# Attention layer with two kinds of heads: how the filling work of the first pair of heads is spread over its units

## The chip, the cores and the metric

The kernel runs on one core of one Trainium2 chip. The metric is device microseconds (us) of one execution, the median of several runs. The core has a matrix engine (TensorE, "PE" in the profile; its weight loads are a row of their own, "PEld"), a vector engine (VectorE, "DVE"), an activation engine (ScalarE, "ACT"), a general engine (GpSimd, "POOL") and a queue engine that issues most transfers ("SP"). Matrix products are written to PSUM, a small memory of banks of 512 columns of fp32 each; the other engines read them from there ("evacuate" them).

## The reference, cut to what matters

One layer over 1024 tokens of width 1024. A normalised and modulated input `u` goes through one projection into queries, keys, values and gates of 16 heads of width 64. Eight heads do stick-breaking attention, eight do forgetting attention; each output is multiplied by a SiLU gate, and an output projection, a residual and a layer norm close the layer. The first pairs of heads, which the change is about, are stick-breaking heads:

```python
z = jnp.einsum('bhqd,bhkd->bhqk', q, k).astype(jnp.float32) * scale
strict = k_pos[None, :] < q_pos[:, None]
log_beta = jax.nn.log_sigmoid(z)
log_keep = jnp.where(strict, jax.nn.log_sigmoid(-z), 0.0)
later = lax.cumsum(log_keep, axis=3, reverse=True) - log_keep
w = jnp.where(strict, jnp.exp(log_beta + later), 0.0)
return jnp.einsum('bhqk,bhkd->bhqd', w.astype(v.dtype), v)
```

A block of 128 queries with number i looks at the keys of blocks 0 to i, so its work grows with i.

## The kernel before, in words

The heads are worked in 8 pairs (p = 0 to 7; pairs 0 to 3 are stick-breaking heads, 4 to 7 forgetting ones). A start phase makes the modulated input and the query, key and gate projections that the first pair needs. Then comes one long loop over 128 *units*: a unit is (pair p, head h of the pair, query block i). In the first four pairs the units run through i = 0 to 7 of head 0, then i = 0 to 7 of head 1. Loop step k does, in this order on TensorE:

1. S k: the scores of unit k (`att_scores`, lines 410 and 411), two matmuls per 512 keys, into the S tile. There is one S tile (two PSUM banks), so S k+1 can only start when ScalarE has read S k twice (lines 430 and 431, the two sigmoids). In step 0 these instructions are put behind the evacuation of the last start product (`last_evac`) by `after(...)`.
2. a first helping of filling work, `fill(want[2 * k + LEAD + 1])`;
3. pv: when both units of a block of 256 queries have been transposed, the product with the values (`att_pv`, line 476), one step after the second of them;
4. T k-2: the transposes of the weights of unit k-2 (`att_transpose`, line 461), i+1 of them, in groups of four per PSUM bank. There are two T banks, taken in turn; a bank is free when ScalarE has copied the high part (line 463) and VectorE has made the low part (line 464);
5. a second helping of filling work, `fill(want[2 * k + LEAD + 2])`.

Between S k and T k-2 of a unit stand two sigmoids on ScalarE, a scan on VectorE that forms the running product of the keep factors (line 436, and line 440 for keys beyond 512) and a product on GpSimd (line 444). GpSimd also splits fetched weights into a high and a low part (lines 124 and 125).

The filling work comes from a chain of generators (`fillers`). Each call of `next(fillers)` issues one small piece; `fill` calls it until the count `done` reaches the wanted number. In pair 0 there are 18 calls (`FILL[0]`):

- call 1 starts the generator and holds no matmul;
- calls 2 to 9 make the values of token blocks 4 to 7 for pairs 0 and 1, two calls for a block, 12 matmuls of 256 columns each (lines 310 to 312);
- call 10 only asks for the weights of the next projection and holds no matmul;
- calls 11 to 18 make the gate projection of pair 1, 6 matmuls of 512 columns in each call (lines 255 to 257);
- beside them, the gate of the residual is made from a sum over partitions: two products (line 715) right behind calls 4 and 5, which use T banks and are evacuated by VectorE (line 716).

The order on TensorE is exactly the program's order (`manual_schedule`). On ScalarE, VectorE, GpSimd and SP the framework orders the instructions itself, by a schedule that it works out from the program and its dependences; edges can be added with `after`. Every tile's reuse waits for all its readers.

`want` is a running sum: each pair's `FILL[p]` calls are shared out over half-units in proportion to a weight. Before, the weight of a unit with query block i is W0 + i + 1 with W0 = 100 in all pairs but the last.

Of the kernel before, what the change touches and what calls it, by code (L numbers as in the profile page):

```python
# [27 lines left out]
def tile_hybrid_layer(  # L28
# [902 lines left out]
    W0 = 100.0  # L931
# [11 lines left out]
    def order(p):  # L943
        if p < 4:
            return [(p, h, i) for h in range(2) for i in range(NB)]
        if p < NPAIR - 1:
            return [(p, h, i) for h in range(2) for i in reversed(range(NB))]
        return [(p, h, i + d) for i in reversed(range(0, NB, 2)) for h in range(2) for d in (1, 0)]
# [1 line left out]
    units = [u for p in range(NPAIR) for u in order(p)]  # L950
    want = [0.0]
    for p in range(NPAIR):
        size = [W0 + u[2] + 1 for u in order(p)]
        if p == NPAIR - 1:
            size = [1] * G7 + [0] * (16 - G7)
        for w in size:
            for _ in range(2):
                want.append(want[-1] + FILL[p] * w / (2 * sum(size)))
# [5 lines left out]
    for k in range(len(units) + LAG + 1):  # L964
        if k < len(units):
# [12 lines left out]
            p, h, i = units[k]  # L978
# [5 lines left out]
        if LAG <= k < len(units) + LAG:  # L984
            u = units[k - LAG]
# [79 lines left out]
```

## Time and profile before

| | before |
|---|---|
| median of 3 runs | 690.2 us (690.01 to 690.37) |
| profiled execution | 689.96 us |
| span from its first to its last instruction | 688.2 us |
| mean granted TensorE clock | 0.998 |
| busy: PE, PEld | 674.0 us (98%), 589.7 us (86%) |
| busy: DVE, ACT, POOL | 453.5 us (66%), 382.1 us (56%), 425.7 us (62%) |

The page and the views that the next part quotes name instructions by engine and line, `out<-in`, with the shape and a count (x2: two in one row); in a timeline row the two numbers are start and duration in us, and a bracket gives the idle time of the engine just before and what released it. A row of the view by stretches has the stretch, its length, the busy time of each engine with the count of instructions, the granted clock and the DMA share.

### The profile page before, as it was taken

What the parts mean: (1) busy time and instruction counts of PE and PEld (TensorE: products, weight loads), DVE (VectorE), ACT (ScalarE), POOL (GpSimd) and SP (SyncE); (2) the same over time, 40 slices, a digit from 0 to 9 for tenths busy, and PEclk for the clock granted to TensorE, in tenths of its full rate; (3) what the DMA queues carried; (4) which work ended last, traced back from release to release, by engine and by line L of the source; (5) the groups of instructions that cost most, each with busy time, mean ns of one, the idle gap of its engine ahead of it and who ended that gap; (6) DMA issues with size and microseconds to landing.
All of it is one profiled execution on the core that took longest, in us unless ns stands there. A gap on an engine that the chain in (4) does not pass through costs nothing.

```text
span 688.2 us, 11786 instructions
## 1 busy us (share of the span) xinstructions
PE 674.0 (98%) x4033; PEld 589.7 (86%) x4033; DVE 453.5 (66%) x924; ACT 382.1 (56%) x862; POOL 425.7 (62%) x555
## 2 busy tenths in 40 slices
PE   8999999999999999999999999999999999999996
PEld 4789898888998888889998888889988889888885
DVE  5985458767657676767675665656665767774645
ACT  5666457856657666666674564655565666531000
POOL 4567978656439565556388897877584364665411
PEclk9999999999999999999999999999999999999999
DMA  8956232112102122112144553454341288143301
GB/s 306 416 233 230 85 108 57 26 40 53 40 9 70 41 55 55 38 47 62 25 136 153 177 160 116 146 163 145 100 143 46 67 293 352 56 155 119 128 32 61
DMA packets 44028, 81.59 MB, mean 119 GB/s; under 512 B 5120, under 2 KB 18752, under 8 KB 43072
## 3 DMA queue, kind: packets, MB, share of 16 engines
q1 hardware_dynamic: 42816, 76.65, 34.0%
q10 hardware_dynamic: 1152, 4.19, 2.2%
q8 instruction: 32, 0.52, 0.3%
q14 instruction: 28, 0.23, 0.1%
HBM read 60.34 MB, written 16.29 MB: 111 GB/s over the span
## 4 chain that ended last, share of the span: by engine, by line
PE 92%; DVE 3%; DMA 2%; POOL 1%; issue 1%; ACT 0%; SPq 0%; POOLq 0%; DVEq 0%
PE m L255 10%; PE pv L476 10%; PE m L256 10%; PE m L257 10%; PE T L461 9%; PE S L411 5%; PE S L410 5%; PE o L848 4%; PE o L846 4%; PE o L847 4%; PE v L310 4%; PE v L312 4%; PE v L311 4%; DMA wss<-in_w_ss_dram 1%; DMA x<-in_x_dram 1%
## 5 line engine op out<-in xcount | busy, mean ns | idle before, releaser
L255 PE MATMUL m<-uh,whi 128*128 128x512 f32 x304 | 126.4, 416 | 0.5 <-DVE kl L243 0.5
L256 PE MATMUL m<-ul,whi 128*128 128x512 f32 x304 | 119.8, 394 | 0.0
L257 PE MATMUL m<-uh,wlo 128*128 128x512 f32 x304 | 119.6, 394 | 0.0
L464 DVE TENSOR_TENSOR pt<-T,pt 128x512 fp32r<-128x512 f32 (+2 forms) x192 | 100.5, 550 | 17.9 <-ACT pt L463 16.8
L444 POOL TENSOR_TENSOR be<-be,kp 128x127 f32<-128x127 f32 (+3 forms) x64 | 77.1, 1205 | 33.5 <-DVE kp L440 23.6
L463 ACT CAST pt<-T 128x512 fp32r<-128x512 f32 (+2 forms) x192 | 85.7, 480 | 16.7 <-PE T L461 13.0
L436 DVE TENSOR_TENSOR_SCAN kp<-kp,floor 128x512 f32<-128x512 f32 (+2 forms) x64 | 65.1, 1018 | 32.1 <-ACT kp L430 31.3
L476 PEld LDWEIGHTS pv<-pt,v 128*128 128x128 f32 (+1 forms) x640 | 77.2, 163 | 4.5 <-DVE pt L464 0.7
L476 PE MATMUL pv<-pt,v 128*128 128x256 f32 (+3 forms) x640 | 80.5, 271 | 0.5 <-DVE pt L464 0.5
L425 POOL TENSOR_SCALAR a<-a,l 128x1024 f32<-128x1024 f32 (+3 forms) x64 | 47.9, 748 | 39.5 <-DVE l L424 25.9
L423 ACT ACTIVATE a<-a,nm 128x1024 f32<-128x1024 f32 (+3 forms) x64 | 49.8, 778 | 34.0 <-DVE nm L417 33.0
L257 PEld LDWEIGHTS m<-uh,wlo 128*128 128x128 f32 x304 | 57.1, 188 | 13.5
L410 PE MATMUL S<-k,q 128*128 128x512 f32 (+5 forms) x192 | 66.5, 348 | 0.2 <-DVE nm L417 0.2
L411 PE MATMUL S<-kl,qz 128*128 128x512 f32 (+5 forms) x192 | 65.5, 342 | 0.0
L255 PEld LDWEIGHTS m<-uh,whi 128*128 128x128 f32 x304 | 57.3, 188 | 9.2 <-DVE kl L243 0.9
L256 PEld LDWEIGHTS m<-ul,whi 128*128 128x128 f32 x304 | 57.4, 189 | 8.0
L497 POOL TENSOR_TENSOR ty<-ty,sg 64x256 f32<-64x256 f32 x64 | 47.4, 741 | 24.6 <-DVE ty L496 12.2
L417 DVE CUSTOM_DVE_ANT_0 a<-S,fb 128x1024 f32<-128x1024 f32 (+3 forms) x64 | 48.3, 755 | 20.4 <-PE S L411 9.8
L430 ACT ACTIVATE kp<-S 128x128 f32<-128x128 f32 (+3 forms) x64 | 41.7, 651 | 31.8 <-PE S L411 28.3
L310 PE MATMUL v<-whi_v,uh 128*128 128x256 f32 (+1 forms) x192 | 56.0, 292 | 0.7 <-DVE kl L243 0.7
L388 ACT CAST qz<-q 64x128 fp32r<-64x128 f32 x128 | 37.4, 295 | 33.0 <-PE S L411 31.9
L312 PE MATMUL v<-wlo_v,uh 128*128 128x256 f32 (+1 forms) x192 | 54.2, 282 | 0.0
(291 smaller groups left out, 1611.5 us busy)
## 6 DMA issues: line engine op xcount, KB each, us to landing
raw<-in_w_qkg_dram SPq DMA_DIRECT2D x38, 256.0 KB, 2.8
wss<-in_w_ss_dram SPq DMA_DIRECT2D x7, 1024.0 KB, 8.3
x<-in_x_dram SPq DMA_DIRECT2D x8, 512.0 KB, 7.3
k<-k SPq DMA_DIRECT2D x32, 128.0 KB, 2.5
wg<-in_w_gate_dram SPq DMA_DIRECT2D x8, 512.0 KB, 4.4
raw_o<-in_w_out_dram SPq DMA_DIRECT2D x16, 256.0 KB, 2.7
fb<-f_dr ACTq DMA_DIRECT2D x8, 512.0 KB, 4.2
wo_dr<-whi_o SPq DMA_DIRECT2D x16, 256.0 KB, 2.5
```

Source lines behind the costliest of these rows:

```text
L255: nc.tensor.matmul(acc, hi[:, c], u_hi[kt][:, s], start=(kt == 0), stop=False)
L256: nc.tensor.matmul(acc, hi[:, c], u_lo[kt][:, s], start=False, stop=False)
L257: nc.tensor.matmul(acc, lo[:, c], u_hi[kt][:, s], start=False, stop=(kt == NB - 1))
L310: nc.tensor.matmul(acc[:, :n], u_hi[kt][:, ts_], hi[:, s], start=(kt == 0), stop=False)
L312: nc.tensor.matmul(acc[:, :n], u_hi[kt][:, ts_], lo[:, s], start=False, stop=(kt == NB - 1))
L410: nc.tensor.matmul(S[:, s, :w], qst[p][h][:, qs], kst[p][h][:, ks], start=True, stop=False)
L411: nc.tensor.matmul(S[:, s, :w], z, klo[p][:, ks], start=False, stop=True)
L436: scan = nc.vector.tensor_tensor_scan(rv, rv, floor[0][:, 512 - n:][:, ::-1], initial=0.0, op0=ALU.mult, op1=ALU.max)
L444: nc.gpsimd.tensor_tensor(be[:, :ke - 1], be[:, :ke - 1], kp[:, 1:ke], op=ALU.mult)
L463: nc.scalar.copy(hi[:, :n, qo:qo + P], t3)
L464: nc.vector.tensor_tensor(lo[:, :n, qo:qo + P], t3, hi.bitcast(F32)[:, :n, qo:qo + P], op=ALU.subtract)
L476: nc.tensor.matmul(acc[:m, q0:256], vt[p][:, kb, h * P:h * P + m], pt[:, kb % 4, q0:], start=start, stop=stop)
```

## The change

One expression: in pair 0 the weight of a unit is 4 + i + 1 in place of 100 + i + 1. Over one head the weights then run from 5 to 12 in place of 101 to 108. The 18 calls of the pair stay, and so do all other pairs.

```diff
     for p in range(NPAIR):
-        size = [W0 + u[2] + 1 for u in order(p)]
+        size = [(W0 if p else 4.0) + u[2] + 1 for u in order(p)]
         if p == NPAIR - 1:
```

`fill` works in whole calls, so the places of the calls follow from the running sums ("a": the helping behind the scores, "b": the helping behind the transposes of the step):

| step k | 0 | 1 | 2 | 3 | 4 | 5 | 6 | 7 | 8 | 9 | 10 | 11 | 12 | 13 | 14 |
|---|---|---|---|---|---|---|---|---|---|---|---|---|---|---|---|
| before, a | 1, 2 | | | | 7 | 8 | 9 | | | | | | 16 | 17 | 18 |
| before, b | 3 | 4 | 5 | 6 | | | 10 | 11 | 12 | 13 | 14 | 15 | | | |
| after, a | 1, 2 | | | 5 | 6 | 7 | 9 | 10 | 11 | | | 14 | 15 | 16 | 18 |
| after, b | | 3 | 4 | | | 8 | | | | 12 | 13 | | | 17 | |

From step 15 on the calls stand where they stood (19 and 20 at 15a, 21 at 15b).

## The prediction

> **What bounds the kernel now.** I read the busy times by stretch first, to see which engine has no room, and looked at the stage of the first pair of heads (92.0 to 132.49 us, from the first score product of unit 0 to that of unit 14). Columns: stretch, its length, busy PE, PEld, DVE, ACT, POOL (instructions), clock, DMA.
>
> ```profile
> 92.00:132.49 40.49, 39.17 (x273) 36.03 (x271) 30.82 (x52) 29.78 (x73) 27.42 (x41) 1.00 0.22 60
> 145.00:300.00 155.00, 154.26 (x962) 137.75 (x961) 104.26 (x172) 99.65 (x225) 90.95 (x128) 1.00 0.17 45
> 300.00:500.00 200.00, 200.00 (x1315) 181.85 (x1315) 129.29 (x303) 117.62 (x284) 145.27 (x168) 1.00 0.40 121
> 500.00:620.00 120.00, 119.26 (x690) 102.98 (x689) 84.61 (x217) 69.96 (x170) 67.81 (x86) 1.00 0.48 161
> ```
>
> TensorE (PE) is busy 39.17 of 40.49 us in this stage and practically always from 145 to 620 us. Its work is the same before and after the change. So any new PE gap here is paid in full at the end, because nothing behind it has room to take it back (0.74 us idle in each of two stretches of 155 and 120 us), and all that can be won is the gaps that stand here now. The second view is the timeline of PE around those gaps, in loop step 7 and 8 (S k: scores of unit k; T k: its transposes; columns: start, us, engine, line).
>
> ```profile
> 111.15 0.39 PE L410 MATMUL S<-k,q 128*128 128x512 f32 x1
> 111.38 0.40 PE L411 MATMUL S<-kl,qz 128*128 128x512 f32 x1
> 112.56 0.84 PE L461 MATMUL T<-ident,be 128*128 128x128 f32 x6 [0.78 <-DVE pt L464]
> 113.16 0.47 PE L255 MATMUL m<-uh,whi 128*128 128x512 f32 x1
> ...
> 114.64 0.22 PE L410 MATMUL S<-k,q 128*128 128x128 f32 x1
> ...
> 114.81 0.75 PE L476 MATMUL pv<-pt,v 128*128 128x256 f32 x5
> 116.10 0.98 PE L476 MATMUL pv<-pt,v 128*64 128x256 f32 x7 [0.54 <-DVE pt L464]
> 116.92 0.93 PE L461 MATMUL T<-ident,be 128*128 128x128 f32 x7
> 117.60 0.48 PE L255 MATMUL m<-uh,whi 128*128 128x512 f32 x1
> ```
>
> Matmul records overlap, so I count from start to start: a 128x512 matmul takes 0.23 (111.15 to 111.38), a call of six 1.48 with the refill behind transposes (113.16 to 114.64), a pv product 0.12 ((116.92-116.10)/7). The gap shown as 0.78 is then 112.56-111.38-0.23 = 0.95, the one shown as 0.54 is 116.10-114.81-5 x 0.117 = 0.70. Both wait for VectorE (DVE), whose rows say why:
>
> ```profile
> 110.29 1.01 DVE L440 TENSOR_TENSOR_SCAN kp<-kp,floor 128x384 f32<-128x384 f32 x1
> ...
> 111.73 0.87 DVE L464 TENSOR_TENSOR pt<-T,pt 128x512 fp32r<-128x512 f32 x2
> ...
> 114.18 1.28 DVE L440 TENSOR_TENSOR_SCAN kp<-kp,floor 128x512 f32<-128x512 f32 x1
> 115.38 0.99 DVE L464 TENSOR_TENSOR pt<-T,pt 128x512 fp32r<-128x512 f32 x2
> ```
>
> T 5 needs a T bank that the low part of T 4 frees, and this stands behind the scan of S 6; pv of block 2 needs the low part of T 5, which stands behind the scan of S 7. These scans start when S 6 and S 7 have run. The most that could be won is 0.95 + 0.70 = 1.65.
>
> **The change, part by part.** It adds and removes no instruction; it moves the calls of the filling generator by the table above. Calls 3 to 8 and 11 to 17 come up to a unit later, calls 1, 2, 9 and 18 stand where they stood. Call 10 holds no matmul, so step 7 loses its only cover and step 8 keeps one.
>
> *Step 0 loses call 3.* Behind S 0 only call 2 is left, and then comes S 1, which needs the single S tile: both sigmoids of unit 0 must have read it.
>
> ```profile
> 92.18 0.33 PE L310 MATMUL v<-v_home,uh 128*128 128x256 f32 x1
> ...
> 93.67 0.28 PE L310 MATMUL v<-whi_v_2b,uh 128*128 128x256 f32 x1
> ...
> 95.09 0.28 PE L410 MATMUL S<-k,q 128*128 128x256 f32 x1
> ```
>
> ```profile
> 93.54 0.58 ACT L240 CAST k<-st_k1b 64x512 fp32r<-64x512 f32 x1 [0.55 <-DVE kl L243]
> 94.14 0.28 ACT L430 ACTIVATE kp<-S 128x128 f32<-128x128 f32 x1
> 94.32 0.27 ACT L431 ACTIVATE be<-S 128x128 f32<-128x128 f32 x1
> ...
> 106.11 0.81 ACT L431 ACTIVATE be<-S 128x768 f32<-128x768 f32 x1
> ...
> 112.73 1.02 ACT L431 ACTIVATE be<-S 128x1024 f32<-128x1024 f32 x1
> ```
>
> ```profile
> 106.96 0.47 PE L410 MATMUL S<-k,q 128*128 128x448 f32 x1
> ...
> 110.14 0.71 PE L461 MATMUL T<-ident,be 128*128 128x128 f32 x5
> 110.60 0.48 PE L410 MATMUL S<-k,q 128*128 128x512 f32 x1
> ```
>
> Call 2 ends at 93.67 (the row there is the first matmul of call 3). ScalarE (ACT) reads S 0 late, because the evacuation of the last start product stands ahead of it, put there in the code (the scores of unit 0 follow last_evac), and ends at 94.32+0.27 = 94.59. From such an end to PE go about 0.05 us: the sigmoid from 106.11 ended at 106.92, S 6 began at 106.96. So S 1 starts at 94.64 where PE is free at 93.67: **+0.97**. Before, call 3 covered it (S 1 at 95.09). Bounds: 0 if ACT took the sigmoids ahead of the evacuation, which the code's order excludes; 1.0 with the whole wait.
>
> *Calls 4 to 8 later, the gate products with 4 and 5.* Each of the steps 1 to 4 still has a call between one S and the next, which hides the sigmoids. The gate products now take their T banks in the order T 0, gate, gate, T 1; call 5 stands ahead of the second, so their evictions (one DVE operation each) are hidden; without that cover it would cost one:
>
> ```profile
> 99.81 0.68 DVE L716 SCALAR_TENSOR_TENSOR gate<-bg,gate 128x512 f32<-128x512 f32 x1
> ...
> 118.23 1.16 DVE L464 TENSOR_TENSOR pt<-T,pt 128x512 fp32r<-128x512 f32 x2 [0.24 <-ACT pt L463]
> ```
>
> T 2 needs the GpSimd (POOL) product of unit 2, which stood behind weight splits that waited for a DMA:
>
> ```profile
> 102.93 0.86 POOL L444 TENSOR_TENSOR be<-be,kp 128x383 f32<-128x383 f32 x1
> ```
>
> ```profile
> 102.27 0.28 PE L310 MATMUL v<-whi_v_2b,uh 128*128 128x256 f32 x1
> ...
> 103.69 0.57 PE L476 MATMUL pv<-pt,v 128*128 128x256 f32 x4
> 104.10 0.49 PE L461 MATMUL T<-ident,be 128*128 128x128 f32 x3
> ```
>
> PE now reaches T 2 without call 7 (103.69-102.27 = 1.42) and 0.97 late: 104.10-1.42+0.97 = 103.65. The product ends at 103.79, with 0.05 on it 103.84: **+0.19**, or 0 if POOL takes it ahead of the splits, which this trace cannot show. I take 0.19, since the DMA that holds POOL does not depend on the calls. What POOL queues behind it (products of units 3 and 4) is needed later.
>
> *Calls 7 and 8 on the other side of T 3, call 10 in step 7.* From S 6 to T 5 the PE order is as before, so the 0.95 gap at T 5 stays: the scan of S 6 still starts when S 6 has run.
>
> *Call 11 from behind T 5 to behind S 8.* On the clock of the old trace, T 5 ends at 113.16 and S 8 follows at once, but the sigmoid of unit 7 reads the S tile until 112.73+1.02 = 113.75: S 8 at 113.80, a new gap of 0.64. Then S 8 (114.81-114.64 = 0.17), call 11 (6 x 0.23 = 1.40) and five pv products (0.59) end at 115.96, before the low part of T 5 is there for 116.10. The old gap of 0.70 shrinks to 0.14 and the pv goes on at 116.10 as before: **0** in sum.
>
> *Call 12 from behind T 6 to behind T 7.* This takes the cover from the T banks.
>
> ```profile
> 119.08 0.28 PE L410 MATMUL S<-k,q 128*128 128x256 f32 x1
> ...
> 119.32 1.04 PE L461 MATMUL T<-ident,be 128*128 128x128 f32 x8
> 120.11 0.48 PE L255 MATMUL m<-uh,whi 128*128 128x512 f32 x1
> ...
> 121.59 0.34 PE L410 MATMUL S<-k,q 128*128 128x384 f32 x1
> ...
> 121.94 1.94 PE L476 MATMUL pv<-pt,v 128*128 128x256 f32 x16
> ...
> 132.49 0.47 PE L410 MATMUL S<-k,q 128*128 128x448 f32 x1
> ```
>
> S 9 starts at 117.60 instead of 119.08, and T 7 could start 0.24 later (119.32-119.08), at 117.84. Its bank is freed by the low part of T 6, which DVE starts at 118.23 (row above); the first of the two takes 0.67 (the one from 115.38 let the pv go on at 116.10): with 0.05 on it 118.95, a gap of 1.11. The second bank comes at 118.23+1.16+0.05 = 119.44, so T 7 ends, half of 120.11-119.32 later, at 119.84, call 12 (1.48) at 121.32, S 10 (121.94-121.59 = 0.35) at 121.67. The old order stood at this pv at 121.94 with call 13 (121.59-120.11 = 1.48) done, the new one still owes it: 121.67-121.94+1.48 = **+1.21**. Bounds: 0 if DVE had T 6's parts out by 117.84, which the ACT copy ahead of it excludes; above by one more call without cover, 1.48. Calls 13 to 17 each stand again between two score products, and at S 14 (132.49 before) the debt is paid and the orders are equal.
>
> The sum: 0.97 + 0.19 + 0 + 1.21 = 2.37. The profiled execution took 689.96, so 692.33, say 692.3; it is 0.24 below the median of 690.2, inside their spread, so the median may come out at 692.5.
>
> **Rivals.**
>
> *Only the first wait stays.* ACT and DVE reorder around S 9 so that T 7 finds its banks free: 689.96+0.97+0.19 = 691.1. For it: DVE was idle 0.24 ahead of T 6's low part, so it follows PE closely. Against it: the transposes themselves end only at 117.60, and copy and subtraction must follow.
>
> *The old gaps close (the other side).* With S 6 later against T 3 and T 4, DVE could take the low parts of T 4 and T 5 ahead of the scans of S 6 and S 7; then 0.95 and 0.70 go, T 7's bank is early too, and the first waits remain: 689.96-1.65+1.16 = 689.5. The decisive point is whether the low part of T 4 stands ahead of the second scan of unit 6 on DVE. Against it: that scan started at 110.29, and T 4 ran only from 110.14 to 110.60, with ACT's copy to follow.
>
> *More room than the gaps show.* Weight loads are busy 36.03/40.49 = 89.0% of this stage, and 181.85/200.00 = 90.9% of the stretch without a gap. At that share the stage would take 36.03/0.909 = 39.6, 0.9 less: 689.1, if the new places of the calls also closed the small losses behind transposes. Against it: as many calls as before stand next to transposes or scores. The Trainium skill (Perfetto Trace Analysis, Identifying the Most-Contended Engine) has such a rule: matmul busy share is no good measure of headroom, the weight-load share is. By it the 0.9 would be the headroom in place of the 1.65 counted from start to start; the trace has gaps with a named cause, so I go by these.
>
> *A further wait.* A call moved once more loses its cover, at S 12 for instance, where the tanh of the gate path enters ACT after call 14: up to one call, 1.48, on top: 693.8.
>
> **How the numbers follow.** My forecast 0.60 (its own range 691.6 to 693.2), only the first wait 0.18, a further wait 0.12, old gaps close 0.06, more room 0.04. The range from 690.2 to 694.0 leaves out the two faster cases and a rest above. A change of 0.2% is 1.38 us, about what a measurement of this kernel tells from none. Slower by more than that: most of 0.60, 0.12, and a little of the second case: 0.73; within it: 0.22; faster: 0.05.
>
> **What would show it.** Right: S 1 starts right behind the sigmoid of unit 0, about 1 us of PE idle with ACT as its releaser; a PE gap of about 0.6 ahead of S 8 and of about 1.1 ahead of T 7 (released by DVE), S 14 some 2.4 us later than 132.49, and the same distance at all later units. Wrong: PE runs through from S 0 to T 4 without a gap; the 0.95 at T 5 shrinks; or S 14 moves by 2.4 and the end doesn't, which would mean room behind that I don't see.

## The result, and the profile after

| | before | after |
|---|---|---|
| median (6 runs each, same chip) | 690.24 us (690.01 to 690.62) | 692.54 us (692.24 to 692.81) |
| span of the profiled execution | 688.2 us | 691.1 us |

The ratio is 1.0034 (95% interval 1.0024 to 1.0044): the changed kernel is 0.34% slower, 2.30 us.

The first view is TensorE's own waits in the changed kernel, from 90 to 150 us (line waiting, releaser, us in total, times, longest):

```profile
PE T L461 <- DVE pt L464: 1.8, 2, 1.0
PE S L410 <- ACT be L431: 1.2, 2, 0.8
```

Before, there was no wait of the scores for the sigmoid in this stage; for VectorE there were two at the transposes, 0.9 together and 0.8 of it at T 5, and one of 0.5 in the pv. Now two score products wait for the sigmoid, the second long wait at the transposes is a new one, and the one in the pv is gone. The timeline of TensorE shows where (start, duration; the idle time in the bracket):

```profile
92.73 0.22 PE L410 MATMUL S<-k,q 128*128 128x128 f32 x1
...
94.27 0.28 PE L312 MATMUL v<-v_home,uh 128*128 128x256 f32 x1
95.37 0.38 PE L410 MATMUL S<-k,q 128*128 128x256 f32 x1 [0.82 <-ACT be L431]
...
104.47 0.49 PE L461 MATMUL T<-ident,be 128*128 128x128 f32 x3
...
113.11 0.40 PE L411 MATMUL S<-kl,qz 128*128 128x512 f32 x1
114.28 0.85 PE L461 MATMUL T<-ident,be 128*128 128x128 f32 x6 [0.78 <-DVE pt L464]
115.53 0.33 PE L410 MATMUL S<-k,q 128*128 128x128 f32 x1 [0.40 <-ACT be L431]
...
117.25 1.56 PE L476 MATMUL pv<-pt,v 128*128 128x256 f32 x12
118.65 0.93 PE L461 MATMUL T<-ident,be 128*128 128x128 f32 x7
119.33 0.37 PE L410 MATMUL S<-k,q 128*128 128x256 f32 x1
119.53 0.28 PE L411 MATMUL S<-kl,qz 128*128 128x256 f32 x1
120.80 1.06 PE L461 MATMUL T<-ident,be 128*128 128x128 f32 x8 [0.98 <-DVE pt L464]
...
135.47 0.36 PE L410 MATMUL S<-k,q 128*128 128x448 f32 x1
...
143.75 0.22 PE L410 MATMUL S<-k,q 128*128 128x128 f32 x1
...
169.31 0.37 PE L410 MATMUL S<-k,q 128*128 128x448 f32 x1
```

S 1 (95.37), S 8 (115.53) and T 7 (120.80) start late, each with the releaser named in its bracket; T 5 waits as before. The last rows are S 14, S 16 and S 22. What these waits stand behind is in the rows of ScalarE, VectorE and GpSimd of the changed kernel:

```profile
94.87 0.28 ACT L430 ACTIVATE kp<-S 128x128 f32<-128x128 f32 x1
95.04 0.27 ACT L431 ACTIVATE be<-S 128x128 f32<-128x128 f32 x1
...
114.46 1.02 ACT L431 ACTIVATE be<-S 128x1024 f32<-128x1024 f32 x1
```

```profile
117.11 1.00 DVE L464 TENSOR_TENSOR pt<-T,pt 128x512 fp32r<-128x512 f32 x2
...
119.95 1.16 DVE L464 TENSOR_TENSOR pt<-T,pt 128x512 fp32r<-128x512 f32 x2 [0.23 <-ACT pt L463]
```

```profile
101.67 0.87 POOL L444 TENSOR_TENSOR be<-be,kp 128x383 f32<-128x383 f32 x1
102.49 1.30 POOL L125 TENSOR_TENSOR wlo<-raw,whi 128x512 fp32r<-128x512 f32 x1
```

Before, this split (the low half of fetched weights) came first and the product followed at 102.93:

```profile
101.63 1.31 POOL L125 TENSOR_TENSOR wlo<-raw,whi 128x512 fp32r<-128x512 f32 x1
```

The sigmoid of unit 0 ends at 95.31 and S 1 starts 0.06 later; the one of unit 7 ends at 115.48 and S 8 starts 0.05 later; the first of the two low parts of T 6 runs from 119.95 for 0.69, to 120.64, and T 7 starts at 120.80. The product of unit 2 on GpSimd now runs ahead of that split, not behind it.

**Where to measure.** S 0 itself starts at 92.01 before and at 92.73 after, though nothing ahead of it was changed; over all profiles here it lies between 91.63 and 92.73. That spread of the start phase is in the spans, so I compare distances inside the stage. Before, the same three later points, S 14, S 16 and S 22, are:

```profile
132.49 0.47 PE L410 MATMUL S<-k,q 128*128 128x448 f32 x1
...
140.88 0.22 PE L410 MATMUL S<-k,q 128*128 128x128 f32 x1
...
166.39 0.37 PE L410 MATMUL S<-k,q 128*128 128x448 f32 x1
```

From S 0 to S 14 it is 40.48 before and 42.74 after (+2.26); to S 16, the first unit of pair 1, 48.87 and 51.02 (+2.15: S 14 now stands behind a call and not behind transposes, which is 0.1 less from there). From S 16 to S 22 it is 25.51 and 25.56, and from S 0 to the end of the span 596.2 (688.2 - 92.01) and 598.4 (691.1 - 92.73). So the whole loss is made in pair 0 and kept to the end. The stretches behind show TensorE as full as before:

```profile
145.00:300.00 155.00, 154.25 (x967) 137.98 (x966) 102.45 (x172) 97.78 (x219) 90.14 (x127) 1.00 0.17 44
300.00:500.00 200.00, 200.00 (x1319) 181.99 (x1318) 130.63 (x302) 119.11 (x287) 145.36 (x168) 1.00 0.39 120
```

### The profile page after: what moved, and what is told of

Its sections match the earlier page's. It is cut to its first block, busy times and chain, and to the rows that moved or that the text cites. A ratio compares the mean times of both kernels' runs of the same rounds, so it can differ in the third digit from the quotient of the medians.

```text
span 691.1 us, 11787 instructions
## 1 busy us (share of the span) xinstructions
PE 675.0 (98%) x4033; PEld 589.7 (85%) x4033; DVE 453.7 (66%) x924; ACT 381.8 (55%) x862; POOL 425.7 (62%) x555
## 4 chain that ended last, share of the span: by engine, by line
PE 93%; DVE 3%; DMA 2%; issue 1%; ACT 1%; SPq 0%; POOL 0%; POOLq 0%; DVEq 0%; ACTq 0%
PE m L255 10%; PE pv L476 10%; PE m L256 10%; PE m L257 10%; PE T L461 9%; PE S L410 5%; PE S L411 5%; PE o L846 4%; PE o L848 4%; PE o L847 4%; PE v L310 4%; PE v L312 4%; PE v L311 4%; DMA wss<-in_w_ss_dram 1%; DMA x<-in_x_dram 1%
```

## The experiments

The theory: the loss is two separate things, S 1 waiting for the sigmoid of unit 0, and S 8 and T 7 waiting because step 7 got the call without a matmul and steps 8 and 9 their calls too late. The rivals: one common cause; another releaser than the one the trace names; or VectorE as a limit that moves along with TensorE. The experiments on the places of calls all write the table of counts (calls done after helping a, after helping b) for steps 0 to 14 in place of the running sums, into the kernel before. For the early part alone:

```diff
+    PLAN = ((2, 2), (2, 3), (3, 4), (5, 5), (6, 6), (7, 8), (9, 10), (10, 11), (11, 12), (12, 13), (13, 14), (14, 15), (16, 16), (17, 17), (18, 18))
+    for k, (a, b) in enumerate(PLAN):
+        want[2 * k + LEAD + 1], want[2 * k + LEAD + 2] = a, b
     want += [want[-1]] * 16
```

The results together. "Stage" is the distance from S 0 to S 16 in the profiled execution against 48.87 before; each kernel was timed in 9 to 11 runs beside the kernel before, on the same chip (33 runs, median 690.06, for the first four; 31 runs, 690.14, for the last four). The ratio stands as it was recorded; it differs from the quotient of the two medians by up to 0.0003.

| kernel | median, us | against before | ratio (95%) | stage | 
|---|---|---|---|---|
| early part alone | 691.14 | +1.08 | 1.0013 (1.0004 to 1.0022) | +1.01 |
| late part alone | 691.20 | +1.14 | 1.0016 (1.0007 to 1.0025) | +1.12 |
| changed, no edge at S 0 | 691.18 | +1.12 | 1.0014 (1.0005 to 1.0023) | +1.15 |
| calls 11 to 15 ahead | 688.62 | -1.44 | 0.9979 (0.9970 to 0.9988) | -1.51 |
| call 3 alone | 691.25 | +1.11 | 1.0016 (1.0007 to 1.0025) | +1.05 |
| changed, no low part of T 6 | 691.68 | +1.54 | 1.0022 (1.0013 to 1.0031) | +1.43 |
| early part and calls ahead | 689.65 | -0.49 | 0.9992 (0.9983 to 1.0001) | -0.47 |
| calls ahead, call 21 too | 688.58 | -1.56 | 0.9977 (0.9967 to 0.9987) | -1.83 |

### The two parts by themselves

The table above holds the early part alone; the late part alone:

```diff
+    PLAN = ((2, 3), (3, 4), (4, 5), (5, 6), (7, 7), (8, 8), (9, 9), (10, 10), (11, 11), (11, 12), (12, 13), (14, 14), (15, 15), (16, 17), (18, 18))
```

> The calls of steps 0 to 5 (3 to 8) stand as in the changed kernel, those from step 6 on as in the kernel before. Theory: only the wait of S 1 for the sigmoid of unit 0 is new (0.98 us in the changed kernel), and the two old gaps at T 5 and in the pv stay: before + 1.0, 691.2. Rival, one cause at S 9 and T 7 for all of the loss: no change from before, 690.2.

> The calls of steps 0 to 5 stand as before, those from step 6 on (10 to 17) as in the changed kernel. Theory: new gaps of 0.64 ahead of S 8 and 1.1 ahead of T 7, the old gap in the pv closes: before + 1.2 to 1.3, 691.5; together with the early part alone the two add up to the whole change, 2.3. Rival, one cause in step 0: no change from before, 690.2.

The TensorE timelines of the two, first the early part, then the late part:

```profile
92.53 0.22 PE L410 MATMUL S<-k,q 128*128 128x128 f32 x1
...
95.16 0.39 PE L410 MATMUL S<-k,q 128*128 128x256 f32 x1 [0.81 <-ACT be L431]
...
114.08 0.85 PE L461 MATMUL T<-ident,be 128*128 128x128 f32 x6 [0.77 <-DVE pt L464]
...
117.63 0.98 PE L476 MATMUL pv<-pt,v 128*64 128x256 f32 x7 [0.55 <-DVE pt L464]
...
142.41 0.22 PE L410 MATMUL S<-k,q 128*128 128x128 f32 x1
```

```profile
91.63 0.22 PE L410 MATMUL S<-k,q 128*128 128x128 f32 x1
...
112.17 0.85 PE L461 MATMUL T<-ident,be 128*128 128x128 f32 x6 [0.78 <-DVE pt L464]
...
113.42 0.33 PE L410 MATMUL S<-k,q 128*128 128x128 f32 x1 [0.40 <-ACT be L431]
...
118.69 1.06 PE L461 MATMUL T<-ident,be 128*128 128x128 f32 x8 [0.98 <-POOL ty L497]
...
141.62 0.22 PE L410 MATMUL S<-k,q 128*128 128x128 f32 x1
```

Each has its own new waits and none of the other's. In the stage they add up: 1.01 + 1.12 = 2.13 against 2.15 for the whole change. The late part alone, +1.14 in the medians, is a little under its forecast of 1.2 to 1.3. One common cause is out. What S 8 waits for is told by the bracket and by its start 0.05 behind the sigmoid; no run takes that sigmoid away. The last bracket names GpSimd for T 7, while the same wait of the same length is put down to VectorE in the changed kernel; which of the two it is has its own experiment below.

### Call 3 alone

```diff
+    PLAN = ((2, 2), (3, 4), (4, 5), (5, 6), (7, 7), (8, 8), (9, 10), (10, 11), (11, 12), (12, 13), (13, 14), (14, 15), (16, 16), (17, 17), (18, 18))
```

> The kernel before with call 3 alone moved from behind S 0 to behind S 1 (step 1 then has calls 3 and 4). Theory: the wait of S 1 belongs to this one call, so this alone costs what the whole early part costs, before + 1.0, 691.1. Rival: the early part's loss is spread over the steps 0 to 5, and this costs half of it or less, 690.6.

It costs 1.05 in the stage, as much as all the moves of the early part (1.01). Together, the moves of the other five calls of that part cost nothing.

### Is it the sigmoid that S 1 waits for?

```diff
-            with after(*last_evac if k == 0 else ()):
+            with after():
                 att_scores(units[k], units[k + 1] if k + 1 < len(units) else None)
```

> The changed kernel without the edge that puts the scores of unit 0 behind the last start evacuation; ScalarE then does the two sigmoids of unit 0 ahead of the second half of that evacuation, some 1.1 us earlier, and nothing changes on PE. Theory: S 1 no longer waits, the changed kernel less 0.98: 691.5, with the gaps at S 8 and T 7 as they were. Rival, S 1 waits for something else (the query copy, the weight splits): no change from the changed kernel, 692.5.

ScalarE's rows in this kernel, and then TensorE's:

```profile
92.91 0.27 ACT L430 ACTIVATE kp<-S 128x128 f32<-128x128 f32 x1
93.08 0.27 ACT L431 ACTIVATE be<-S 128x128 f32<-128x128 f32 x1
...
93.76 0.58 ACT L240 CAST k<-st_k1b 64x512 fp32r<-64x512 f32 x1 [0.23 <-DVE kl L243]
```

```profile
92.23 0.22 PE L410 MATMUL S<-k,q 128*128 128x128 f32 x1
...
93.77 0.28 PE L312 MATMUL v<-v_home,uh 128*128 128x256 f32 x1
93.89 0.28 PE L410 MATMUL S<-k,q 128*128 128x256 f32 x1
...
142.25 0.22 PE L410 MATMUL S<-k,q 128*128 128x128 f32 x1
```

The sigmoids now run ahead of the second half of the start evacuation, and S 1 follows call 2 without a gap. The stage is 51.02 - 50.02 = 1.00 shorter than in the changed kernel, with TensorE's order untouched. So the wait is the sigmoid's, and it is late because of the edge. The edge holds back ScalarE's part of step 0 alone, not the score product: before, with the edge, S 0 ran at 92.01 and the second half of the evacuation only at 93.54.

### Is it VectorE's low part that T 7 waits for?

In the changed kernel, with the low part of unit 6's weights left out (zeros in its place, so the output of one block of queries has less precision):

```diff
+            if u == (0, 0, 6):
+                nc.gpsimd.memset(lo.bitcast(F32)[:, :n, qo:qo + P], 0.0)
+            else:
-            nc.vector.tensor_tensor(lo[:, :n, qo:qo + P], t3, hi.bitcast(F32)[:, :n, qo:qo + P],
-                                    op=ALU.subtract)
+                nc.vector.tensor_tensor(lo[:, :n, qo:qo + P], t3, hi.bitcast(F32)[:, :n, qo:qo + P],
+                                        op=ALU.subtract)
```

> The changed kernel; the low part of the transposed weights of unit 6 (pair 0, head 0) is left out, GpSimd writes zeros in its place, so T 7's banks are free after the ACT copy. Theory: T 7 starts some 0.8 us earlier, and the changed kernel gets 0.8 us shorter, 691.6. Rival, T 7 waits for the GpSimd product of unit 7: the zeros are more work on GpSimd, and T 7 starts no earlier, 692.5 or more.

```profile
119.10 0.37 PE L410 MATMUL S<-k,q 128*128 128x256 f32 x1
...
119.84 1.06 PE L461 MATMUL T<-ident,be 128*128 128x128 f32 x8 [0.25 <-POOL pt L465]
```

```profile
119.11 0.97 ACT L463 CAST pt<-T 128x512 fp32r<-128x512 f32 x2
```

```profile
117.05 2.00 POOL L444 TENSOR_TENSOR be<-be,kp 128x1023 f32<-128x1023 f32 x1
...
119.38 0.42 POOL L465 MEMSET pt<- 128x384 f32 x1
119.76 0.72 POOL L500 TENSOR_TENSOR ty<-ty,sg 64x256 f32<-64x256 f32 x1
```

From S 9 to T 7 it is 0.74 in place of 1.47 (120.80 - 119.33), and the stage is 0.72 shorter (51.02 - 50.30). The low part it is, for 0.73 of the 1.15 that T 7 waited. GpSimd's product of unit 7 ended at 119.05 and was not the limit, and neither was its gate product (line 497, here line 500), which the bracket in the late part alone names: it runs from 119.76 to 120.48, and T 7 starts at 119.84. So a bracket that names GpSimd for this wait names the last signal, not the cause; in the kernel without the edge, the view of waits puts the 0.8 at T 5 down to a weight split of GpSimd, where the other kernels name VectorE.

The 0.25 that is left was not tried by a run. T 7 now starts in the middle of ScalarE's two copies of T 6 (119.11 to 120.08). The first of them takes 0.59, to 119.70, and T 7 follows 0.14 later; in the changed kernel T 7 starts about 0.15 behind the end of the first low part of T 6, and T 5 as much behind that of T 4 (113.46 + 0.67 = 114.13, 114.28). That fits the copy. But the write of the zeros ends at 119.80, 0.04 ahead of T 7, and by the trace alone it is not excluded.

### Calls ahead of the waits

```diff
+    PLAN = ((2, 3), (3, 4), (4, 5), (5, 6), (7, 7), (8, 8), (9, 10), (11, 11), (12, 12), (13, 13), (14, 14), (15, 15), (16, 16), (17, 17), (18, 18))
```

> The kernel before with calls 11 to 15 one helping earlier, from behind the transposes of steps 7 to 11 to behind the scores of the same steps. Theory: a call then stands ahead of T 5, the pv of block 2 and T 7, where PE waits for DVE; the gaps of 0.95 and 0.70 shrink to 0.18 (S 8 for the sigmoid of unit 7) and 0.14: before - 1.3 to - 1.5, 688.8. Rival, DVE falls behind by as much as PE comes earlier: no change, 690.2.

> The early calls (3 to 8) as in the changed kernel, the late ones (11 to 15) behind the scores of steps 7 to 11, so that the call without a matmul no longer leaves step 7 without cover. Theory: the two parts do not touch each other; + 1.0 for S 1, - 1.5 for the closed gaps: 689.7. Rival, the late gain needs the early calls where they were: 690.2 or more.

The last one takes the same late part behind the early part of the changed kernel. The version with the calls ahead, by TensorE's timeline:

```profile
92.16 0.22 PE L410 MATMUL S<-k,q 128*128 128x128 f32 x1
...
112.91 0.39 PE L257 MATMUL m<-uh,wlo 128*128 128x512 f32 x1
113.14 0.82 PE L461 MATMUL T<-ident,be 128*128 128x128 f32 x6
113.94 0.33 PE L410 MATMUL S<-k,q 128*128 128x128 f32 x1
...
115.67 1.55 PE L476 MATMUL pv<-pt,v 128*128 128x256 f32 x12
...
139.52 0.22 PE L410 MATMUL S<-k,q 128*128 128x128 f32 x1
```

No bracket is left in these rows, and the view of TensorE's waits from 90 to 150 us is empty. T 5 starts right behind call 11 (113.14 = 112.91 + 0.23); S 8 has a rest of 0.2 (113.94 - 113.14 - 0.60). So VectorE did not fall behind by as much as TensorE came earlier: with a call ahead of each of these places, none waits for it. With the early part of the changed kernel it comes out at -0.47 in the stage, which is 1.01 - 1.51 = -0.50: the two parts do not touch each other. The ratio of this combined version does not exclude 1, so by the medians alone it cannot be told from the kernel before.

The next version adds one line to this table:

```diff
+    want[2 * 15 + LEAD + 1] = 21
```

> The version with calls 11 to 15 behind the scores of steps 7 to 11, and call 21 moved from behind T 13 to ahead of it in step 15. Theory: the last gap of the pair, 0.31 ahead of T 13 (shown as 0.15), closes too: before - 1.8, 688.4. Rival: S 16 then follows T 13 at once and waits for the sigmoid of unit 15 in its turn: before - 1.5, 688.7.

Its distance to S 16 is 139.22 - 92.18 = 47.04, 0.32 less than without the line, as forecast, and no wait of S 16 shows. But from S 16 to S 22 it takes 25.64 in place of 25.51, so 0.19 is left at S 22; why was not looked into. In the medians the two stand at -1.44 and -1.56, which these runs cannot tell apart, so the 1.8 of the forecast is not borne out. Both beat the kernel before, and through it the changed one, beside which they were not timed.

## Why the prediction was right

Forecast 692.3, measured 692.54; forecast difference 2.37, measured 2.30 in the medians and 2.26 from S 0 to S 14. The two waits that make up the loss were named in advance, with their releasers, and runs show the cause of the first whole and of the second for 0.73 out of 1.15. That the sum is so close is in part luck: one term was 0.19 too large, and smaller ones made up 0.08 of it. By its steps:

- *Step 0 loses call 3, 0.97.* In the changed kernel call 2 ends at 94.27 + 0.12 = 94.39, S 1 starts at 95.37: 0.98. Call 3 alone and the kernel without the edge show that this one move and this one sigmoid are the cause.
- *T 2 and the product of unit 2, 0.19.* It was 0: T 2 started at 104.47 without a wait, because the framework put the product ahead of a weight split (101.67 and 102.49). This was the lower bound, and the term of the sum that was sized wrongly; why the schedule of GpSimd changed stays open. From S 0 to T 5 it takes 21.55 and before 20.55, so the whole early loss is 1.00.
- *T 5 stays at 0.95.* 114.28 - 113.11 - 0.23 = 0.94.
- *Call 11 behind S 8, 0 in sum.* S 8 starts 0.65 behind the end of T 5 (115.53 - 114.28 - 0.60; forecast 0.64), the wait in the pv is gone (forecast 0.14 left), and from T 5 to T 6 it takes 118.65 - 114.28 = 4.37, before 116.92 - 112.56 = 4.36. The sum came true, though not quite as counted: S 8 and call 11 took 1.72 behind the wait (117.25 - 115.53) in place of the 1.57 counted, and this used up the 0.14 that the pv was to wait.
- *Call 12 behind T 7, 1.21.* The gap is 120.80 - 119.53 - 0.12 = 1.15 against 1.11 counted. From T 6 to S 14 it takes 16.82, before 15.57, so this step cost 1.25. Part of the rest is the way from the end of the low part to T 7, about 0.15 where the sum had 0.05. With T 2 at 0, the sum to S 14 would have been 2.18; it was 2.26 (1.00 + 0.01 + 1.25).
- *Nothing behind takes it back.* From S 16 to S 22 the distance moved by 0.05, and the later stretches are as full as before.

The rivals: that only the first wait stays fell with T 7's 0.98 in the trace; that the old gaps close fell with T 5's 0.94; no further wait came. For the headroom, the 0.9 from the weight-load share was too low: the version with calls ahead won 1.51 in the stage, near the 1.65 counted from start to start. The estimate of 0.9 had taken the 90.9% of another stretch as the most that the weight-load share can be; with the calls ahead, 36.08 us of weight loads stand in the 39.05 us from S 0 to S 14, which is 92.4%. The rule of the Trainium skill (Perfetto Trace Analysis, Identifying the Most-Contended Engine) takes the weight-load share, beside the share of peak operations, and not the matmul busy share, as the measure of headroom. The runs here do not decide on that rule, only on the 0.9 drawn from it: most of what was to be won stood in two gaps with a named releaser.

## What to carry to other kernels

Where filling work stands matters only at places that it has to cover, between a producer and the product that waits for it: here five of six early moves cost nothing together, and one cost 1.05. A weight that looks fair by size says nothing of that, so go through the order step by step and ask at each wait which call stands ahead of it. A helping that only fetches covers nothing, and counting it as one can leave a step bare. Where an engine is full to the end, as TensorE was here, a gap opened in one stage reaches the end (2.26 at S 14, about 2.2 at the end of the span), and its cost could be summed from start times in the old trace to within 0.2.

## What the runs showed of the hardware

The start phase, written the same in all these kernels but for the edge, placed S 0 anywhere from 91.63 to 92.73 us, so the span of one execution cannot resolve a change of 1 us, while a distance inside a stage held far better: 25.50 to 25.56 from S 16 to S 22 in the nine profiles with the same order of calls there. And a gap's bracket understates it: at T 5 it says 0.78 where the start times say 0.94, because the matmul ahead is drawn 0.40 long, and in rows without a wait the next starts after 0.23. From the end of an instruction to the TensorE instruction that it released it took 0.05 to 0.06 for a score product behind a sigmoid, and about 0.15 for T 5 and T 7 behind a low part.
